# Latent attention by banks of scores, with queries on the partitions of its outputs

## The chip, the core and the metric

One core of a Trainium2 chip runs the whole program. The metric is the device time of one execution in microseconds (us). The kernel before was run three times without a profile and once more with one.

## What is computed

A two-part transformer block on 256 tokens of width 1024, in float32: feed-forward layers, a stick-breaking mixer, cross attention on 256 memory tokens, a state-space mixer, sparse attention. The change lies in the mixer of layer 1 of the first part, a causal attention over latents with 16 heads of 96 query/key features and 64 value features:

```python
def _causal_softmax_attention(q, k, v):
    scale = q.shape[-1] ** -0.5
    def block(args):                      # 128 queries at a time
        q_blk, i = args
        sc = jnp.einsum('bqhd,bkhd->bhqk', q_blk, k) * scale
        causal = k_pos[None, :] <= q_pos[:, None]
        p = jax.nn.softmax(jnp.where(causal, sc, -jnp.inf), axis=-1)
        return jnp.einsum('bhqk,bkhd->bqhd', p, v)
...
def _mla_mixer(...):
    c_q, c_kv, k_r = jnp.split(h @ w_in, ...)
    q = (_rmsnorm(c_q, q_lora_g) @ w_uq)      # 16 heads x 96
    kv = (_rmsnorm(c_kv, kv_lora_g) @ w_ukv)  # 16 heads x (64 + 64)
    ...                                       # norms, rotary part
    return _causal_softmax_attention(q, k, v) @ w_out
```

## The kernel before

Tokens stand in two tiles of 128 (`T` = 0, 1). A weight is loaded as raw float32 (`stage`, DMA on SP's queue), split into a high part on ACT (line 126) and a low part on DVE (line 127), and each product with a weight is three one-pass matmuls (`mm3`, lines 150 to 152). Small products (scores, transposes, probabilities times values) are plain float32 matmuls, which the trace shows as two records for one product and one record for one transpose.

In `mla` the heads go in four chunks of four (`c` = 0 to 3). `heads(c)` makes the chunk's queries, keys and values, `turn` transposes queries and keys (line 858), `attend(c)` is the attention, and `kv(c)` makes one head of the keys and values for the cross attention that follows; it shares nothing with `attend`. `attend(c)` is followed in the program by `heads(c + 1)`, `turn` and `kv(c + 1)`, and at the end come `kv(3)` and `out_linear`, the product with `mla_w_out` (tiles `acc`). The order of instructions on each engine isn't the program's: the tile framework's planner sets it when the program is built, from modelled times and from when buffers come free. So matmuls of `heads`, `kv` and `attend` stand mixed on PE, and each engine then runs its list strictly in that order.

`attend` before, for each `T` and each head `j`: one score product into a PSUM tile of tag C (two of them); DVE adds the mask and takes the row maximum into SBUF tile `s_` (line 920, three buffers); DVE forms minus maximum times scale (line 922); ACT takes the exponential with its row sum (line 924); DVE takes the reciprocal (926) and divides the probabilities (927); `transpose_p` transposes one block (T = 0) or two (T = 1) on PE into a tile of tag B (line 659), and ACT copies it to SBUF (661); one or two products with the values as stationary operand, 64 columns wide, give 64 features by 128 queries in tile `o` (line 931). After four heads `split` writes the high and low parts `oh`, `ol` (lines 192, 193), which `out_linear` reads.

Of the kernel before, what the change touches and what calls it, by code (L numbers as in the profile page):

```python
# [12 lines left out]
AF = mybir.ActivationFunctionType  # L13
ALU = mybir.AluOpType
# [3 lines left out]
P = 128  # L18
# [11 lines left out]
class Net:  # L30
# [743 lines left out]
    def mla(self, fin):  # L774
        nc, tc, a = self.nc, self.tc, self.a
        preps = self.preps()
        w_in, w_uq, w_ukv = a["mla_w_in"][0], a["mla_w_uq"][0], a["mla_w_ukv"][0]
        with tc.tile_pool(name=self.nm("mla"), bufs=1) as pl:
            def T_(shape, name, dt=F32, bufs=1, tag=None):
                return self.lined(pl, shape, dt, tag=tag or name, name=self.nm(name), bufs=bufs)  # L780

            TT = lambda o, x, y, op: nc.vector.tensor_tensor(out=o, in0=x, in1=y, op=op)
# [23 lines left out]
            def cols(T):  # L806
                return slice(T * P, (T + 1) * P)
# [45 lines left out]
            oh, ol = self.o_tiles()  # L853
# [54 lines left out]
                    to_T(qn, qT, T, nc.vector.tensor_copy)  # L908

            def attend(c, qT, kT, vn, rq, *_):  # L910
                for T in range(2):
                    nk = P * (T + 1)
                    po = self.psum(f"D{T + 1}", "o")
                    mask = self.m_c2 if T else self.m_c
                    for j in range(4):
                        sc = self.psum("C", "sc")
                        nc.tensor.matmul(sc[:, 0:nk], qT[:, j, cols(T)], kT[:, j, 0:nk], start=True, stop=True)
                        mx = self.small(2)
                        s_ = T_([P, 256], "s_", bufs=3)
                        nc.vector.tensor_tensor_reduce(out=s_[:, 0:nk], in0=sc[:, 0:nk], in1=mask, scale=1.0, scalar=-3.0e38,  # L920
                                                       op0=ALU.add, op1=ALU.max, accum_out=mx[:, 0:1])
                        nc.vector.tensor_scalar(out=mx[:, 1:2], in0=mx[:, 0:1], scalar1=rq[:, T, j:j + 1], scalar2=-1.0, op0=ALU.mult, op1=ALU.mult)
                        ssum = self.small(1)
                        nc.scalar.activation(s_[:, 0:nk], s_[:, 0:nk], AF.Exp, scale=rq[:, T, j:j + 1], bias=mx[:, 1:2], accum_out=ssum)
                        rec = self.small(1)
                        nc.vector.reciprocal(rec, ssum)
                        nc.vector.tensor_scalar(out=s_[:, 0:nk], in0=s_[:, 0:nk], scalar1=rec, scalar2=None, op0=ALU.mult)
                        pT = self.transpose_p(s_, T + 1, pl, "pT", 2)
                        o = po[(j % 2) * 64:(j % 2) * 64 + 64, (j // 2) * P:(j // 2 + 1) * P]
                        for b in range(T + 1):  # L930
                            nc.tensor.matmul(o, vn[b][:, j, :], pT[:, b, :], start=b == 0, stop=b == T)
                    self.split(po[:, 0:256].rearrange("p (k t) -> p k t", k=2), oh[:, 2 * c:2 * c + 2, cols(T)], ol[:, 2 * c:2 * c + 2, cols(T)])

            kv(0)
            hs = heads(0)
# [1 line left out]
            for c in range(4):  # L937
                attend(c, *hs)
                if c < 3:
                    hs = heads(c + 1)  # L940
                    turn(*hs)
                if c < 2:
                    kv(c + 1)
# [703 lines left out]
```

## Time and profile before

| what | value |
|---|---|
| runs without a profile | 2251.57, 2252.95, 2255.41 us, median 2252.95 |
| profiled execution, its own time | 2254.93 us |
| its span in the trace | 2253.2 us, so 1.73 us lie around the span |
| granted TensorE clock, mean | 0.996 |
| busy, share of the span | PE 98%, PE weight loads 82%, DVE 71%, ACT 57%, POOL 3% |
| stretch with the attention | about 866 to 968.5 us after the span's start |

PE is the matmul unit and PEld its weight loads, which overlap it. A record of PE is longer than the time that it takes in a stream, since the matmuls are pipelined: where the text speaks of a price in a stream, it is the distance from start to start.

### The profile page before, as it was taken

The page shows a single profiled execution, that of the slowest core. Times are in us where ns is not written, and L with a number is a line of the kernel's source. Part 1 is how long each engine was busy: PE and PEld are TensorE (multiplying, and loading weights), DVE is VectorE, ACT ScalarE, POOL GpSimd, SP SyncE. Part 2 cuts the span into 40 slices and gives each one's busy share as a digit, 9 for nine tenths or more (in the row PEclk, how much of TensorE's full clock was granted, in tenths as well). Part 3 has the DMA queues.
Part 4 walks back from the last instruction along what each step waited for, and adds up shares of the span by engine and source line. Part 5 has one row for each costly group of instructions (what it writes and reads, how often), then busy time and mean ns, then how long its engine had stood idle before and what let it go on. Part 6 is the DMA issues. An engine that isn't in the chain of part 4 may idle for free.

```text
span 2253.2 us, 32357 instructions
## 1 busy us (share of the span) xinstructions
PE 2209.4 (98%) x11697; PEld 1842.9 (82%) x11697; DVE 1591.2 (71%) x3496; ACT 1275.7 (57%) x2864; POOL 74.2 (3%) x112
## 2 busy tenths in 40 slices
PE   8999999999999998999999999999999999999999
PEld 6887767788888886777888888887888888778887
DVE  6788666798766677776767656777568565867566
ACT  6755566655665566765554555455555555455553
POOL 0010000000000001100000000000000000000000
PEclk9999999999999999999999999999999999999999
DMA  6775544467567543344565655656555554527552
GB/s 210 240 232 201 179 140 169 134 216 263 183 217 256 194 138 130 119 169 131 176 198 187 207 186 185 241 187 227 187 174 194 196 190 161 178 94 246 187 180 85
DMA packets 280988, 415.94 MB, mean 185 GB/s; under 512 B 18662, under 2 KB 211324, under 8 KB 279804
## 3 DMA queue, kind: packets, MB, share of 16 engines
q1 hardware_dynamic: 275744, 400.87, 53.6%
q10 hardware_dynamic: 5084, 13.00, 1.6%
q8 instruction: 92, 1.51, 0.3%
q14 instruction: 68, 0.56, 0.1%
HBM read 400.07 MB, written 13.76 MB: 184 GB/s over the span
## 4 chain that ended last, share of the span: by engine, by line
PE 83%; DVE 9%; ACT 3%; issue 1%; DMA 1%; POOL 1%; ACTq 0%; SPq 0%; DVEq 0%; POOLq 0%
PE gate L160 11%; PE up L160 11%; PE acc L150 9%; PE acc L151 9%; PE acc L152 9%; PE gate L162 6%; PE up L162 6%; DVE wlo L127 4%; PE proj L152 3%; PE proj L151 3%; PE proj L150 2%; PE up L150 2%; PE up L152 2%; PE up L151 2%; ACT whi L126 1%; PE xT L177 1%
## 5 line engine op out<-in xcount | busy, mean ns | idle before, releaser
L126 ACT ACTIVATE whi<-raw 128x512 fp32r<-128x512 f32 (+1 forms) x1452 | 816.2, 618 | 409.3 <-PE up L160 175.9
L127 DVE TENSOR_TENSOR wlo<-raw,whi 128x512 fp32r<-128x512 f32 (+1 forms) x1452 | 927.7, 678 | 107.1 <-ACT whi L126 69.4
L160 PE MATMUL gate<-x,whi 128*128 128x512 f32 x1200 | 294.0, 392 | 0.0
L160 PE MATMUL up<-x,whi 128*128 128x512 f32 x1200 | 290.6, 390 | 0.1
L150 PE MATMUL acc<-whi,hh 128*128 128x512 f32 x704 | 276.0, 392 | 2.2 <-ACT hh L192 2.2
L151 PE MATMUL acc<-wlo,hh 128*128 128x512 f32 x704 | 275.3, 391 | 0.0
L152 PE MATMUL acc<-whi,hl 128*128 128x512 f32 x704 | 274.5, 390 | 0.0
L167 DVE TENSOR_TENSOR sg<-gate,sg 128x256 f32<-128x256 f32 x150 | 63.5, 423 | 279.8 <-ACT sg L166 279.6
L160 PEld LDWEIGHTS up<-x,whi 128*128 128x128 f32 x1200 | 221.6, 188 | 43.9 <-DVE h L167 0.3
L160 PEld LDWEIGHTS gate<-x,whi 128*128 128x128 f32 x1200 | 221.5, 188 | 44.0 <-DVE sg L167 0.2
L162 PEld LDWEIGHTS gate<-x,wlo 128*128 128x128 f32 x1200 | 157.7, 191 | 8.2
L162 PE MATMUL up<-x,wlo 128*128 128x256 f32 x1200 | 160.5, 283 | 0.0
L162 PE MATMUL gate<-x,wlo 128*128 128x256 f32 x1200 | 160.2, 282 | 0.0
L162 PEld LDWEIGHTS up<-x,wlo 128*128 128x128 f32 x1200 | 154.9, 191 | 4.5
L150 PE MATMUL proj<-whi,x 128*128 128x512 f32 (+2 forms) x400 | 157.7, 394 | 0.1
L151 PE MATMUL proj<-wlo,x 128*128 128x512 f32 (+2 forms) x400 | 155.9, 390 | 0.0
L152 PE MATMUL proj<-whi,x 128*128 128x512 f32 (+2 forms) x400 | 155.1, 388 | 0.4 <-DVE x L193 0.3
L152 PEld LDWEIGHTS acc<-whi,hl 128*128 128x128 f32 x704 | 132.2, 188 | 28.3 <-DVE hl L193 0.4
L150 PEld LDWEIGHTS acc<-whi,hh 128*128 128x128 f32 x704 | 132.5, 188 | 27.8 <-ACT hh L192 2.6
L151 PEld LDWEIGHTS acc<-wlo,hh 128*128 128x128 f32 x704 | 132.5, 188 | 24.5
L360 ACT ACTIVATE sg<-sg 128x256 f32<-128x256 f32 x150 | 62.5, 416 | 81.0 <-DVE sg L297 78.8
L192 ACT ACTIVATE hh<-h 128x512 fp32r<-128x512 f32 x75 | 47.5, 634 | 104.5 <-DVE h L297 104.5
(730 smaller groups left out, 3007.4 us busy)
## 6 DMA issues: line engine op xcount, KB each, us to landing
raw<-in_ffn_w_dram SPq DMA_DIRECT2D x176, 512.0 KB, 4.7
raw<-in_ffn_post_w_gu_dram SPq DMA_DIRECT2D x88, 512.0 KB, 4.8
raw<-in_ffn_w_dram SPq DMA_DIRECT2D x44, 1024.0 KB, 4.9
raw<-in_ffn_pre_w_gu_dram SPq DMA_DIRECT2D x84, 512.0 KB, 5.2
raw<-in_ffn_pre_w_down_dram SPq DMA_DIRECT2D x22, 1024.0 KB, 5.4
raw<-in_ffn_post_w_down_dram SPq DMA_DIRECT2D x22, 1024.0 KB, 4.9
raw<-in_xmem_wkv_dram SPq DMA_DIRECT2D x16, 1024.0 KB, 4.9
raw<-in_sbg_w_in_dram SPq DMA_DIRECT2D x10, 1024.0 KB, 5.1
```

The costliest lines, as they stand in the source:

```text
L126: self.last_hi = nc.scalar.activation(hi[:, s], raw[:, s], AF.Copy)
L127: self.last_lo = nc.vector.tensor_tensor(out=lo[:, s], in0=raw[:, s], in1=hi[:, s].bitcast(F32), op=ALU.subtract)
L150: nc.tensor.matmul(out, xh, wh, start=first, stop=False)
L151: nc.tensor.matmul(out, *a, start=False, stop=False)
L152: nc.tensor.matmul(out, *b, start=False, stop=last)
L160: mm(out, ws(k)[0], x2[:, k].rearrange("p a t -> p (a t)"), start=k == 0, stop=False)
L162: mm(out[:, 256:512], ws(k)[1], x2[:, k, 0, :], start=False, stop=k == n - 1)
L167: self.nc.vector.tensor_tensor(out=d, in0=ps[:, 256:512], in1=d, op=ALU.add)
L177: nc.tensor.transpose(pt[:, j * P:(j + 1) * P], src[:, (b + j) * P:(b + j + 1) * P], self.ident)
L192: self.nc.scalar.activation(hi, src, AF.Copy)
L360: nc.scalar.activation(d, d, AF.Silu)
```

## The change

All of it is in `attend`. Scores of four heads (T = 0, 128 keys each) or two heads (T = 1, 256 keys each) go into one bank of 512 columns: one bank for T = 0 and two for T = 1. Mask and maximum are still taken head by head, the scaled maxima of a bank in one instruction. The exponentials are still one for each head. The probabilities aren't divided; four transposes fill one bank, which one copy of 512 columns moves to SBUF. In the product with the values the probabilities are now the stationary operand (128 columns) and the values move (64 columns), so that `po` has queries on its partitions. Per T there is one reciprocal of four sums and one multiplication of `po` by it into SBUF tile `on`, and `split_T` transposes `on` (two transposes into a tile of tag B) and splits it. `s_` goes from three buffers of 256 columns to two of 512, `pT` from two of 256 to two of 512.

```diff
                 for T in range(2):
                     nk = P * (T + 1)
                     po = self.psum(f"D{T + 1}", "o")
                     mask = self.m_c2 if T else self.m_c
-                    for j in range(4):
+                    ssum = self.small(4)
+                    for j0, n in ((0, 2), (2, 2)) if T else ((0, 4),):
                         sc = self.psum("C", "sc")
-                        nc.tensor.matmul(sc[:, 0:nk], qT[:, j, cols(T)], kT[:, j, 0:nk], start=True, stop=True)
-                        mx = self.small(2)
-                        s_ = T_([P, 256], "s_", bufs=3)
-                        nc.vector.tensor_tensor_reduce(out=s_[:, 0:nk], in0=sc[:, 0:nk], in1=mask, scale=1.0, scalar=-3.0e38,
-                                                       op0=ALU.add, op1=ALU.max, accum_out=mx[:, 0:1])
-                        nc.vector.tensor_scalar(out=mx[:, 1:2], in0=mx[:, 0:1], scalar1=rq[:, T, j:j + 1], scalar2=-1.0, op0=ALU.mult, op1=ALU.mult)
-                        ssum = self.small(1)
-                        nc.scalar.activation(s_[:, 0:nk], s_[:, 0:nk], AF.Exp, scale=rq[:, T, j:j + 1], bias=mx[:, 1:2], accum_out=ssum)
-                        rec = self.small(1)
-                        nc.vector.reciprocal(rec, ssum)
-                        nc.vector.tensor_scalar(out=s_[:, 0:nk], in0=s_[:, 0:nk], scalar1=rec, scalar2=None, op0=ALU.mult)
-                        pT = self.transpose_p(s_, T + 1, pl, "pT", 2)
-                        o = po[(j % 2) * 64:(j % 2) * 64 + 64, (j // 2) * P:(j // 2 + 1) * P]
-                        for b in range(T + 1):
-                            nc.tensor.matmul(o, vn[b][:, j, :], pT[:, b, :], start=b == 0, stop=b == T)
-                    self.split(po[:, 0:256].rearrange("p (k t) -> p k t", k=2), oh[:, 2 * c:2 * c + 2, cols(T)], ol[:, 2 * c:2 * c + 2, cols(T)])
+                        for j in range(n):
+                            nc.tensor.matmul(sc[:, j * nk:(j + 1) * nk], qT[:, j0 + j, cols(T)], kT[:, j0 + j, 0:nk], start=True, stop=True)
+                        mx = self.small(8)
+                        s_ = T_([P, 512], "s_", bufs=2)
+                        for j in range(n):
+                            ks = slice(j * nk, (j + 1) * nk)
+                            nc.vector.tensor_tensor_reduce(out=s_[:, ks], in0=sc[:, ks], in1=mask, scale=1.0, scalar=-3.0e38,
+                                                           op0=ALU.add, op1=ALU.max, accum_out=mx[:, j:j + 1])
+                        nc.vector.scalar_tensor_tensor(out=mx[:, 4:4 + n], in0=mx[:, 0:n], scalar=-1.0, in1=rq[:, T, j0:j0 + n], op0=ALU.mult, op1=ALU.mult)
+                        for j in range(n):
+                            ks = slice(j * nk, (j + 1) * nk)
+                            nc.scalar.activation(s_[:, ks], s_[:, ks], AF.Exp, scale=rq[:, T, j0 + j:j0 + j + 1], bias=mx[:, 4 + j:5 + j],
+                                                 accum_out=ssum[:, j0 + j:j0 + j + 1])
+                        pt = self.psum("B", "pT")
+                        for j in range(4):
+                            nc.tensor.transpose(pt[:, j * P:(j + 1) * P], s_[:, j * P:(j + 1) * P], self.ident)
+                        pT = T_([P, 4, P], "pT", bufs=2)
+                        nc.scalar.activation(pT, pt.rearrange("p (k t) -> p k t", k=4), AF.Copy)
+                        for j in range(n):
+                            for b in range(T + 1):
+                                nc.tensor.matmul(po[:, (j0 + j) * 64:(j0 + j + 1) * 64], pT[:, j * (T + 1) + b, :], vn[b][:, j0 + j, :], start=b == 0, stop=b == T)
+                    rec = self.small(4)
+                    nc.vector.reciprocal(rec, ssum)
+                    on = T_([P, 4, 64], "on", bufs=2)
+                    TT(on, po[:, 0:256].rearrange("p (h d) -> p h d", h=4), rec[:, :, None].to_broadcast([P, 4, 64]), ALU.mult)
+                    self.split_T(on.rearrange("p h d -> p (h d)"), 2, oh[:, 2 * c:2 * c + 2, cols(T)], ol[:, 2 * c:2 * c + 2, cols(T)])
```

## Rows read from the trace of the kernel before

**Rows 1.** The page: busy time of each engine; the chain that ended last.
```profile
PE 2209.4 (98%) x11697; PEld 1842.9 (82%) x11697; DVE 1591.2 (71%) x3496; ACT 1275.7 (57%) x2864; POOL 74.2 (3%) x112
...
PE 83%; DVE 9%; ACT 3%; issue 1%; DMA 1%; POOL 1%; ACTq 0%; SPq 0%; DVEq 0%; POOLq 0%
```

**Rows 2.** Busy time in the attention's stretch: PE, PEld, DVE, ACT, POOL (instructions), clock, DMA.
```profile
866.00:968.50 102.50, 97.32 (x515) 72.60 (x516) 77.12 (x283) 70.77 (x199) 13.76 (x11) 0.98 0.31 106
```

**Rows 3.** Groups by line, 866 to 968.5 us: busy us, mean ns | idle before, releasers.
```profile
L931 PE MATMUL o<-pT,vn 128*64 128x128 f32 x96 | 16.1, 289 | 0.6 <-ACT pT L661 0.4
...
L917 PEld LDWEIGHTS sc<-kT,qT 96*128 96x128 f32 x64 | 10.5, 202 | 2.3 <-DVE sm L920 0.7 <-DVE sm L922 0.5 <-DVE qT L859 0.2
L661 ACT ACTIVATE pT<-pT 128x128 f32<-128x128 f32 (+1 forms) x32 | 10.3, 330 | 11.2 <-PE pT L659 10.7
...
L931 PEld LDWEIGHTS o<-pT,vn 128*64 128x64 f32 x96 | 9.1, 135 | 9.1 <-ACT pT L661 6.9 <-issue 1.1 <-ACT whi L126 0.9
...
L922 DVE TENSOR_SCALAR sm<-sm,rq 128x1 f32<-128x1 f32 x32 | 6.2, 206 | 0.0
...
L926 DVE RECIPROCAL sm<-sm 128x1 f32<-128x1 f32 x32 | 5.1, 159 | 1.2 <-ACT s__1391_8747 L924 0.3 <-ACT s__1671_9715 L924 0.3 <-ACT s__1692_9769 L924 0.2
...
L193 DVE TENSOR_TENSOR ol<-o,oh 128x256 fp32r<-128x256 f32 x8 | 3.4, 420 | 0.7 <-ACT oh L192 0.7
...
L637 PE MATMUL kTm<-ident,kn 128*128 128x128 f32 x10 | 2.1, 289 | 1.6 <-DVE kn L634 1.6
```

**Rows 4.** Line 927 alone in the same stretch: DVE busy (instructions), clock, DMA.
```profile
866.00:968.50 102.50, 10.13 (x32) 0.98 0.31 106
```

**Rows 5.** Timeline of PE, chunk 0, T = 1: start, length, instructions.
```profile
881.97 0.40 PE L150 MATMUL proj<-whi,x 128*128 128x512 f32 x1
882.30 0.65 PE L931 MATMUL o<-pT,vn 128*64 128x128 f32 x4
882.88 0.44 PE L659 MATMUL pT<-ident,s__1377_8711 128*128 128x128 f32 x2
883.08 0.48 PE L151 MATMUL proj<-wlo,x 128*128 128x512 f32 x1
883.39 0.40 PE L152 MATMUL proj<-whi,x 128*128 128x512 f32 x1
883.62 0.40 PE L150 MATMUL proj<-whi,x 128*128 128x512 f32 x1
```

**Rows 6.** Timeline of PE, value products: one alone, eight, and eight of another attention.
```profile
939.83 0.27 PE L931 MATMUL o<-pT,vn 128*64 128x128 f32 x1
...
965.34 1.02 PE L931 MATMUL o<-pT,vn 128*64 128x128 f32 x8
...
2011.17 1.05 PE L1109 MATMUL o<-pT,vn 128*128 128x128 f32 x8
2011.98 0.48 PE L150 MATMUL acc<-whi,oh 128*128 128x512 f32 x1
```

**Rows 7.** Timeline of PE: 64 moving columns (line 503); four transposes (line 177).
```profile
227.74 2.00 PE L503 MATMUL mix<-gn,swT 128*128 128x64 f32 x16 [0.37 <-DVE gn L578]
...
980.44 0.66 PE L177 MATMUL xT<-ident,x 128*128 128x128 f32 x4
```

**Rows 8.** Single lines with min/median/max ns: a 128-column weight load, a 512-column copy.
```profile
L503 PEld LDWEIGHTS mix<-gn,swT x32: 186/192/192, 227.7 to 245.1; 128*128 128x128 f32 x32
...
L522 ACT ACTIVATE qT<-qkT x2: 574/586/599, 258.7 to 265.2; 128x512 f32<-128x512 f32 x2
```

**Rows 9.** Timeline of PE: transposes that waited for divided probabilities.
```profile
875.49 0.30 PE L659 MATMUL pT<-ident,s__1341_8626 128*128 128x128 f32 x1 [1.32 <-DVE s__1341_8626 L927]
...
941.18 0.41 PE L659 MATMUL pT<-ident,s__1584_9445 128*128 128x128 f32 x2 [0.70 <-DVE s__1584_9445 L927]
```

**Rows 10.** Timeline of ACT and of PE: the last `oh` and the first `acc`.
```profile
966.39 0.38 ACT L192 ACTIVATE oh<-o 128x256 fp32r<-128x256 f32 x1 [0.22 <-PE o L931]
```
```profile
968.46 0.39 PE L150 MATMUL acc<-whi,oh 128*128 128x512 f32 x1
```

## The prediction

> **What bounds the kernel now.** I read the page first. PE is busy 98% of the span, and 83% of the chain that ended last is PE's [rows 1]; so an edit counts by what it does to PE's stream, and work taken from DVE or ACT counts only where PE waits for it. Next, the busy times of the stretch that holds `attend`, 866 to 968.5 us: PE 97.3 of 102.5 us, DVE 77.1, ACT 70.8 [rows 2]. The reader should not take 97.3 for useful time. A record lasts longer than its place in a stream: an undisturbed one-pass matmul of 512 columns follows its neighbour after 0.23 us (883.39 to 883.62) and is 0.40 long [rows 5]; a value-product record costs (1.02 − 0.27)/7 = 0.107 us [rows 6], where 0.27 is the length of one record alone [rows 6]. Hence the third view, groups by shape, for the idle time ahead of weight loads, and the fourth, PE's own timeline.
>
> The timeline shows what the averages hide [rows 5]. From 881.97 to 883.39 PE does one large matmul (0.23), four value records (4 × 0.107 = 0.43), two transposes (0.21) and one large matmul (0.23): 1.10 us of work in 1.42 us. The 0.32 us lost lie at seams: 0.10 before the value records (0.33 − 0.23), which wait for ACT's copy; 0.15 after them (0.58 − 0.43); 0.07 to 0.08 after the transposes. The weight loads of line 931 have 9.1 us of idle time ahead of them in the stretch, 6.9 put down to that copy; those of the scores have 2.3 [rows 3]. So what this stretch loses on PE it loses largely at visits of small matmuls between large ones, and the change is about how many visits there are.
>
> **The change, part by part (PE first).** Before there are 8 heads × 4 chunks = 32 visits each for transposes and value products, and up to 32 for scores. After, three banks × 4 chunks = 12 of each, and 8 more for turning `on`.
>
> *Value products.* Before, 32 × (0.10 + 0.15) = 8.0 us of seams; the 9.1 us of idle time ahead of the same loads is the cross-check. After, 12 visits. The 0.15 behind them stands after tiles that use 64 columns of the array; behind the 128-column products of the other attention the next large matmul follows eight records after 0.81 us, no later than 8 × 0.107 [rows 6], so I drop it. The wait ahead I raise from 0.10 to 0.25, because one copy now moves 512 columns, 0.59 us [rows 8] instead of 0.33 on the mean [rows 3]. That leaves 12 × 0.25 = 3.0: a gain of 5.0, with 8.0 as the upper end (no wait left) and below zero as the lower (the slower rival).
>
> *Transposes of the probabilities.* Their number stays 48. Visits go from 32 to 12 + 8 = 20: 12 × 0.07 = 0.8 us gained.
>
> *Scores.* The same matmuls; a bank's scores need no tile to come free between heads. Of the 2.3 us ahead of those loads, 1.2 are put down to DVE's lines 920 and 922, which free the tile; I take 0.7, between 0 and 2.3.
>
> *Added transposes.* 2 × 2 × 4 = 16 records, by the four of line 177 at (0.66 − 0.27)/3 = 0.13 us [rows 7], or 0.107 back to back: 1.7 to 2.1, and I take 1.7 lost, their seams being counted above.
>
> *Turned operands.* The 96 value records now load 128 columns and move 64 where they loaded 64 and moved 128. The nearest row with just that form, line 503, does 16 records in 2.00 us: (2.00 − 0.27)/15 = 0.115 each [rows 7], so 96 × 0.008 = 0.8 lost. If the longer load showed in full it would be (192 − 135) ns × 96 = 5.5 us [rows 8, 3]; the other end is 0.4, from 0.111 at the eight records of line 1109 [rows 6]. I take 0.8, since line 503 is a stream and not a single duration. [...]
>
> *DVE and ACT.* DVE loses 6.2 (line 922) + 5.1 (line 926) [rows 3] + 10.1 (line 927) [rows 4] = 21.4 us and gains 12 × 0.16 (scaled maxima, taken as long as a reciprocal [rows 3]) + 8 × 0.16 + 8 × 0.42 (a 128×256 read of PSUM, as line 193 [rows 3]) = 6.6: 14.8 us of 77.1 less. ACT's copies go from 10.3 [rows 3] to 12 × 0.59 = 7.0 us. The exponentials and maxima stay. All this is under PE's stream, which covers it; it counts only through waits. PE stood 1.6 us ahead of the `kTm` transposes for DVE's `kn`, which queues among the attention's instructions [rows 3]; I take 0.7 of it, between 0 and 1.6. The 1.32 and 0.70 us waits for divided probabilities [rows 9] lose their cause in line 927, but the transposes now wait for the bank's last exponential instead of the head's own; I count nothing, with 2.0 as the upper end. If the cover were gone, DVE's saving would be worth its 14.8 us; nothing in PE's 97.3 says so.
>
> *New waits.* The reciprocal waits for the fourth exponential, the product into `on` for the last value record; behind it on DVE stand `wlo` splits that feed large matmuls. The two new transposes wait on PE for `on`, and whatever the planner put behind them waits too. `s_` has two buffers, so the second bank of T = 1 waits until the transposes of T = 0 have read theirs. No DMA is added or moved. At the end, the last `oh` is written at 966.39 and `acc` starts at 968.46 [rows 10]; its first tile can run chunks 0 to 2, 36 large matmuls or 8 us, before it needs chunk 3, so a last chunk that ends a few us later is covered.
>
> The sum: 5.0 + 0.8 + 0.7 − 1.7 − 0.8 + 0.7 = 4.7 us. The profiled execution took 2254.93 us (span 2253.2 and 1.73 around it) and would take 2250.2; it lies 2.0 above the median, so against 2252.95 the forecast is 2248.2 us, 0.21% less. Everything behind the stretch starts with `acc`, so I see nothing that gives the gain back later.
>
> **Rivals.** *More gain.* PE's waits in the stretch shrink to the upper ends: 8.0 + 0.8 + 2.3 − 1.7 − 0.4 + 1.6 + 2.0 = 12.6 us, 2240.4. For it: DVE has 15 us less in a stretch where it is busy 75% of the time. Against: the copies and exponentials stay in series on ACT.
>
> *No change: the longer weight loads show.* 5.5 instead of 0.8 takes the whole 4.7: 2252.9. For it, the durations; against, line 503's stream [rows 7]. The same time comes out if the waits ahead of the value records grow to 0.64 us a visit (0.25 + 4.7/12), about one 512-column copy.
>
> *Slower: PE blocks at each bank.* PE runs a fixed list. Where a bank's transposes or value products stand too early in it, PE waits for up to four exponentials and a copy, and no large matmul behind them may pass. The two waits of 1.32 and 0.70 us are this mechanism with one head [rows 9]. With 12 banks the change is slower than before by 0.2% once the mean extra wait exceeds (4.7 + 4.5)/12 = 0.77 us a bank; at the 1.32 us already seen it costs 15.8 − 4.7 = 11.1 us, 2264. Against: matmuls of `heads` and `kv` are there to be put between, and a bank has fewer points at which plan and chip can part.
>
> **How the numbers follow.** 0.2%, 4.5 us, is about what a measurement of this kernel can tell from no change. The forecast (gain of 2 to 8 us) has 0.54, and since 4.7 lies hardly above the bound I split it 0.32 faster, 0.22 same. More gain: 0.13, faster. No change: 0.13, same. Slower: 0.20. So 0.45 faster, 0.35 same, 0.20 slower. The range goes to 2240.5, which leaves out a sliver of the second case, and to 2258, which takes in the start of the slower one, up to a mean wait of 0.8 us a bank: some 0.17 is left out. The likeliest case's own range is 2245 to 2251.
>
> **What would show it.** Right: value records in 12 groups of 8 or 16 where the planner lets them, starting about 0.11 us apart; the idle time ahead of their loads falling from 9.1 to about 3 us; lines 922, 926 and 927 gone from DVE, whose busy time in the stretch falls by about 15 us; `acc` beginning some 5 us earlier against the stretch's start. Wrong: single waits of over 0.8 us on PE ahead of transposes or value products in most banks (slower); value records 0.16 us apart (no change); or a stretch that is shorter by 5 us and a span that isn't, which would mean a wait behind 968 that I don't see.

## The result and the profile after

| kernel | runs | median us | range | ratio to the kernel before, 95% interval |
|---|---|---|---|---|
| before, beside the next row | 4 | 2253.15 | 2251.57 to 2255.41 | |
| changed | 4 | 2269.8 | 2268.07 to 2271.52 | 1.0070 [1.0059, 1.0082] |

The change costs 16.7 us, 0.7%: slower, and outside the range forecast. The profiled execution took 2268.07 us, its span is 2266.1. Two lines of the changed kernel's page, the busy times and the chain that ended last:

```profile
PE 2218.0 (98%) x11713; PEld 1852.0 (82%) x11713; DVE 1584.2 (70%) x3428; ACT 1272.6 (56%) x2844; POOL 73.7 (3%) x112
...
PE 83%; DVE 9%; ACT 4%; DMA 2%; issue 1%; POOL 1%; SPq 0%; ACTq 0%; DVEq 0%; POOLq 0%
```

Against [rows 1] DVE is 7.0 us less busy and PE 8.6 us more, with 16 instructions more. The next view is the busy time of the attention's stretch, now 868 to 977 us, and of three pieces of it (columns as in [rows 2]):

```profile
868.00:977.00 109.00, 98.30 (x531) 83.72 (x532) 67.46 (x215) 67.55 (x178) 12.88 (x11) 0.92 0.29 100
...
881.80:885.30 3.50, 3.50 (x15) 3.21 (x15) 2.26 (x8) 2.17 (x6) 0.00 (x0) 0.51 0.25 93
909.20:916.00 6.80, 6.11 (x28) 5.71 (x27) 2.02 (x5) 4.66 (x13) 1.65 (x1) 0.50 0.18 68
946.70:950.10 3.40, 3.40 (x16) 3.40 (x16) 1.03 (x3) 1.94 (x7) 1.39 (x1) 0.50 0.00 0
```

On PE the stretch holds as many records as before and 16 transposes more. DVE's time fell from 77.1 to 67.5 us: line 927 [rows 4] and the waits for it [rows 9] are gone. The granted clock fell from 0.98 to 0.92: beside the spell at the start that both kernels have, PE runs three times at half of the full clock (granted 0.51, 0.50 and 0.50 in the three pieces above), 17.1 us in all with that first spell, where before had 3.4.

The groups of the same stretch, to be held against [rows 3]:

```profile
L939 PE MATMUL o<-vn,pT 128*128 128x64 f32 x96 | 15.3, 313 | 3.6 <-ACT pT L936 3.6
...
L177 PE MATMUL xT<-ident,on 128*128 128x128 f32 x16 | 3.2, 283 | 1.6 <-DVE on L782 1.6
L637 PE MATMUL kTm<-ident,kn 128*128 128x128 f32 x10 | 2.1, 289 | 1.7 <-DVE kn L634 1.7
...
L939 PEld LDWEIGHTS o<-vn,pT 128*128 128x128 f32 x96 | 14.6, 227 | 5.8 <-ACT pT L936 5.6
L920 PEld LDWEIGHTS sc<-kT,qT 96*128 96x128 f32 x64 | 9.8, 200 | 0.9 <-DVE qT L859 0.2
...
L936 ACT ACTIVATE pT<-pT 128x512 f32<-128x512 f32 x12 | 7.2, 597 | 7.7 <-PE pT L934 7.5
L193 DVE TENSOR_TENSOR ol<-xT,oh 128x256 fp32r<-128x256 f32 x8 | 3.3, 416 | 2.2 <-ACT oh L192 2.1
```

Idle time ahead of the value products' weight loads fell from 9.1 to 5.8 us, that ahead of the scores' from 2.3 to 0.9. But PE itself, which stood 0.4 us for the copies before, stands 3.6 us for them and 1.6 us for `on`. The timeline of PE shows where, in chunk 1, and for comparison chunk 3 with the first `acc` (start, length):

```profile
905.93 0.55 PE L934 MATMUL pT<-ident,s__1416_8955 128*128 128x128 f32 x2
907.17 1.10 PE L939 MATMUL o<-vn,pT 128*128 128x64 f32 x8 [0.69 <-ACT pT L936]
908.79 0.44 PE L177 MATMUL xT<-ident,on 128*128 128x128 f32 x2 [0.52 <-DVE on L782]
909.06 0.96 PE L934 MATMUL pT<-ident,s__1426_8991 128*128 128x128 f32 x4
910.71 1.97 PE L939 MATMUL o<-vn,pT 128*128 128x64 f32 x8 [0.69 <-ACT pT L936]
912.47 1.06 PE L934 MATMUL pT<-ident,s__1431_9012 128*128 128x128 f32 x4
913.18 0.67 PE L150 MATMUL q<-whi,cqh 128*128 128x384 f32 x1
...
967.59 1.00 PE L939 MATMUL o<-vn,pT 128*128 128x64 f32 x8
968.40 0.47 PE L152 MATMUL proj<-whi,x 128*128 128x512 f32 x1
...
976.97 0.40 PE L150 MATMUL acc<-whi,oh 128*128 128x512 f32 x1
```

The planner put transposes, value products and turning of a bank one behind the other, with no large matmul between. From 905.93 to 913.18 PE waits three times for what it has just produced to go through ACT or DVE. In that piece the clock drops, and the eight records that take 1.00 us in chunk 3 take 1.97. Chunks 0 and 2 have the same sequence (waits of 0.52 and 0.69 us up to 881.47, of 0.69, 0.52 and 0.69 up to 946.45), each followed by a drop. In chunk 3 `proj` matmuls lie between and there is no wait.

The view of PE's waits in the stretch has one large row besides (us in total, times, longest):

```profile
PE qkT L858 <- DVE qn L782: 3.6, 2, 1.8
PE o L939 <- ACT pT L936: 3.6, 6, 0.7
PE qkT L858 <- ACT whi L126: 3.4, 1, 3.4
PE kTm L637 <- DVE kn L634: 1.7, 4, 0.6
PE xT L177 <- DVE on L782: 1.6, 3, 0.5
```

The third row is the wait ahead of the stretch's first transpose. The others add up to 10.5 us, where before has 4.4. The two waits of 1.8 us stand ahead of the turning of the next chunk's queries; before has none there (the first of these turnings starts at 918.20 before, without a wait):

```profile
925.29 1.05 PE L858 MATMUL qkT<-ident,qn 128*96 128x128 f32 x8 [1.84 <-DVE qn L782]
```

From the last `q` matmul to this turning it takes 5.1 us before (from 913.09) and 5.6 after (from 919.72). Before, value products and transposes of probabilities fill part of that time; after, they have been done earlier and only `proj` and `qkT` matmuls stand in it. No drop of the clock follows either of these two waits.

From the first `qkT` transpose of the stretch (866.61 before, 868.18 after) to the first `acc` (968.46 in [rows 10], 976.97 here) it takes 101.85 us before and 108.79 after. That explains 6.9 of the 12.9 us by which the span grew. The rest, 6.0 us, lies in stages that the diff doesn't touch; it would be larger, had these two executions been at the lower clock equally long there (before for 6.8 us twice, at 26.8 and 1992.9, the changed kernel for 3.4 once, at 195.8). The page's groups of the second feed-forward product, of before and then of the changed kernel (busy us, mean ns):

```profile
L150 PE MATMUL acc<-whi,hh 128*128 128x512 f32 x704 | 276.0, 392 | 2.2 <-ACT hh L192 2.2
L151 PE MATMUL acc<-wlo,hh 128*128 128x512 f32 x704 | 275.3, 391 | 0.0
L152 PE MATMUL acc<-whi,hl 128*128 128x512 f32 x704 | 274.5, 390 | 0.0
```
```profile
L150 PE MATMUL acc<-whi,hh 128*128 128x512 f32 x704 | 279.2, 397 | 1.9 <-ACT hh L192 1.9
L152 PE MATMUL acc<-whi,hl 128*128 128x512 f32 x704 | 279.0, 396 | 0.0
L151 PE MATMUL acc<-wlo,hh 128*128 128x512 f32 x704 | 278.7, 396 | 0.0
```

The same 2112 matmuls got 5 ns longer each, 11.1 us of records. `small(4)` is a new size in the pool of small tiles: 12 buffers of 32 bytes, which move every tile allocated behind it, `hh` among them, by 384 bytes of each partition (`hh` from byte 140800 to 141184). So there are two questions: is the place of the tiles really a cause, and what makes the stretch longer, the edit or the order in which the planner wrote it out?

### The profile page after: what moved, and what is told of

It is laid out like the page before. It is cut to its first block, busy times and chain, and to the rows that moved or that the text cites. A ratio compares the mean times of both kernels' runs of the same rounds, so it can differ in the third digit from the quotient of the medians.

```text
span 2266.1 us, 32261 instructions
## 1 busy us (share of the span) xinstructions
PE 2218.0 (98%) x11713; PEld 1852.0 (82%) x11713; DVE 1584.2 (70%) x3428; ACT 1272.6 (56%) x2844; POOL 73.7 (3%) x112
## 4 chain that ended last, share of the span: by engine, by line
PE 83%; DVE 9%; ACT 4%; DMA 2%; issue 1%; POOL 1%; SPq 0%; ACTq 0%; DVEq 0%; POOLq 0%
PE gate L160 11%; PE up L160 11%; PE acc L150 9%; PE acc L151 9%; PE acc L152 9%; PE gate L162 6%; PE up L162 6%; DVE wlo L127 4%; PE proj L152 3%; PE proj L150 3%; PE proj L151 2%; PE up L152 2%; PE xT L177 2%; PE up L150 2%; ACT whi L126 2%; PE up L151 1%
```

## The experiments

Each ratio is to runs of the kernel before on the same chip (medians 2253.2 to 2254.1 us).

| kernel | median us | ratio, 95% interval | stretch us | half clock, spells that touch it, us |
|---|---|---|---|---|
| before | | | 101.9 | 3.4 |
| changed | 2269.8 | 1.0070 [1.0059, 1.0082] | 108.8 | 17.1 |
| before, moved by 384 bytes | 2263.9 | 1.0046 [1.0033, 1.0058] | 102.1 | 3.4 |
| before, moved by 128 | 2264.1 | 1.0046 [1.0029, 1.0062] | 102.0 | 3.4 |
| before, moved by 256 | 2253.9 | 1.0000 [0.9991, 1.0009] | 101.9 | 3.4 |
| before, moved by 512 | 2253.6 | 1.0000 [0.9991, 1.0008] | 101.8 | 3.4 |
| changed, realigned | 2259.9 | 1.0026 [1.0017, 1.0035] | 108.8 | 17.1 |
| realigned, waits filled | 2260.4 | 1.0027 [1.0018, 1.0037] | 109.2 | 3.4 |
| realigned, copy in halves | 2257.5 | 1.0015 [1.0006, 1.0024] | 105.4 | 10.2 |
| changed, other order | 2251.5 | 0.9989 [0.9980, 0.9998] | 100.6 | 3.4 |
| changed, one bank ahead | 2254.5 | 1.0003 [0.9995, 1.0012] | 104.3 | 6.8 |
| turned outputs only | 2250.6 | 0.9984 [0.9975, 0.9993] | 99.5 | 3.4 |
| banks only | 2248.5 | 0.9977 [0.9962, 0.9992] | (94.1) | 6.8 |
| banks only, heads 0, 2, 1, 3 | 2249.1 | 0.9982 [0.9973, 0.9991] | (94.3) | 3.4 |

Stretch and half clock are read from the one profiled execution of each kernel. The five with the order of before agree (101.8 to 102.1 and 3.4 us), and so do the changed kernel and its realigned form, which have one order (108.8 and 17.1). With banks only, `acc` begins ahead of the last two banks, so those two stretches aren't like the others.

**The place of the tiles.** The kernel before with the pad tile behind the small ones made larger; the order on PE, DVE and ACT stays:

```diff
-        tc.nc.gpsimd.memset(self.pad.tile([P, 24], F32, name="pad"), 0.0)
+        tc.nc.gpsimd.memset(self.pad.tile([P, 120], F32, name="pad"), 0.0)
```

> The kernel before with the pad tile widened by 384 bytes, so that every tile allocated behind it stands where it stands in the changed kernel; the order on PE, DVE and ACT is the same as before. Layout theory (the new size of small tiles moved hh and hl, and matmuls that load them got slower): 8 to 11 us more, 2261 to 2264, and the mean of the acc<-whi,hh records goes from 392 to about 397 ns. Attention theory (all of the loss is in the attention's stretch): 2253, means as before.

It took 10.1 us more and its `acc` groups read as in the changed kernel:

```profile
L150 PE MATMUL acc<-whi,hh 128*128 128x512 f32 x704 | 279.2, 397 | 1.8 <-ACT hh L192 1.8
L152 PE MATMUL acc<-whi,hl 128*128 128x512 f32 x704 | 279.1, 396 | 0.0
L151 PE MATMUL acc<-wlo,hh 128*128 128x512 f32 x704 | 278.5, 396 | 0.0
```

Then the same with `[P, 152]`, `[P, 88]` and `[P, 56]`: 512, 256 and 128 bytes.

> The kernel before with every tile behind the small ones moved by 512 bytes of each partition instead of 384; the instructions and their order are those of the kernel before. Theory A (what costs is that the operands of the three-pass products stand at another place within 512 bytes): no difference, 2251 to 2255 us, and the three lines of acc at 392, 391 and 390 ns as before. Rival B (any move of the tiles costs): 2260 us or more, as for the move by 384.

> The kernel before with the same tiles moved by 256 bytes. Theory A in its plain form (any place other than a multiple of 512 costs the same): 2262 to 2266 us and acc at about 396 ns, as for the move by 384. Rival B (the remainder by 256 or 128 decides, or the move alone): 2251 to 2255 us and acc at 392 ns if 256 is enough.

> The kernel before with the same tiles moved by 128 bytes; moved by 256 and by 512 it took its old time, moved by 384 ten us more. Theory A (an odd multiple of 128 bytes costs, whatever the distance): 2261 to 2267 us, acc at 396 to 397 ns. Rival B (only the remainder 384 of 512, or that one distance, costs): 2251 to 2256 us, acc at 390 to 393 ns.

512 and 256 cost nothing (2253.6 and 2253.9 against 2254.1 us), 128 costs 10 us again (2264.1 against 2253.8). So distance is not what counts, and my plain form, a multiple of 512, fell with the move by 256. What these four moves agree with is an odd multiple of 128 bytes against an even one; no other distance was run.

The counterpart, the changed kernel with the pad at `[P, 56]`, which puts `hh` at an even multiple again (141312) and leaves the order as it was:

> The changed kernel with the pad tile widened by 128 bytes, so that hh and hl start at a multiple of 512 bytes again; order the same as in the changed kernel. Layout theory: 8 to 11 us less than the changed kernel, 2259 to 2262, acc records back at 390 to 392 ns, and the attention's stretch still about 7 us longer than before with its spells of half clock. Attention theory: 2270, no change.

9.9 us came back, the `acc` groups read 393, 392 and 391 ns, and the stretch stayed as it was, clock included. So the place of the tiles is about 10 of the 16.7 us, and 6 remain, in the stretch.

**The edit or its order.** The small tiles of four cut from tiles of eight, a size that the kernel already had:

```diff
-                    ssum = self.small(4)
+                    ssum = self.small(8)[:, 0:4]
...
-                    rec = self.small(4)
+                    rec = self.small(8)[:, 0:4]
```

> The changed kernel whole, with one difference: its two four-wide small tiles are cut from the eight-wide ones that were there before. So no tile moves against the kernel before, and the planner, which counts another set of buffers, writes another order of the same instructions: in chunks 0 and 3, and in parts of 1 and 2, projection matmuls now stand between a bank's transposes, its value products and the turning. Theory A (the edit is sound, and the loss of the realigned changed kernel, 2259.9 us against 2253.8 before, is the planner's order: waits at the hand-offs between the banks and the half clock that follows them): fewer hand-off waits on TensorE between 868 and 975 us, at most one half-clock spell beyond the one at the start of the stretch, and 2245 to 2251 us, for the bank half alone gained 5.3 us and the turning half 3.2. Rival B (banks and turned outputs together are too much, whatever the order): 2257 to 2261 us, half-clock spells as in the realigned one.

Theory A held, though 2251.5 us lies just above its range. The stretch is 8.2 us shorter than in the realigned kernel, with the same instructions in another order. Its timeline in chunk 1:

```profile
904.76 0.38 PE L177 MATMUL xT<-ident,on 128*128 128x128 f32 x2
904.98 0.60 PE L934 MATMUL pT<-ident,s__1426_8991 128*128 128x128 f32 x4
905.34 0.42 PE L151 MATMUL q<-wlo,cqh 128*128 128x384 f32 x1
...
906.33 1.10 PE L939 MATMUL o<-vn,pT 128*128 128x64 f32 x8
```

Five `q` matmuls (the first at 905.34) stand where the changed kernel waited. Over the stretch PE waits 0.9 us for the copies instead of 3.6, and no drop of the clock follows the one at the start. Against the kernel before it is 1.8 us faster by the medians; the interval of the ratio goes from 0.5 to 4.5 us.

**Waits and clock.** Work added into the waits of the realigned kernel, into columns of the output bank that nothing reads, behind each bank's transposes:

```diff
+                        for _ in range(6):
+                            nc.tensor.matmul(po[:, 256:512], cqh[:, 0, 0:P], cqh[:, 1, :], start=True, stop=True)
```

> The realigned changed kernel (2259.9 us) with work added: behind each of the 12 banks' transposes six one-pass matmuls of 256 columns into the unused half of the output bank, whose result nothing reads. They are 72 matmuls of some 0.11 us, 7.7 us of TensorE work in all if nothing covers them. Theory A (waits at the hand-offs and the half clock that follows them): the added work runs in waits that are there anyway, and where it does the granted clock stays up; the time is 2254 to 2262 us, the half-clock spells beyond the first of the stretch fewer than three. Rival B (the stretch is bound by TensorE's own work): the added work comes on top, 2266 to 2269 us.

The whole stretch, realigned and then filled, and what replaced the wait of 0.69 us in chunk 1:

```profile
864.80:973.60 108.80, 98.19 (x531) 83.60 (x532) 67.42 (x214) 67.33 (x177) 12.88 (x11) 0.92 0.30 100
```
```profile
864.70:973.90 109.20, 99.98 (x591) 84.60 (x592) 66.92 (x214) 66.96 (x177) 12.89 (x11) 0.99 0.30 99
```
```profile
905.07 0.60 PE L934 MATMUL pT<-ident,s__1426_9015 128*128 128x128 f32 x4
905.43 0.96 PE L936 MATMUL o<-cqh 128*128 128x256 f32 x6
906.36 1.10 PE L941 MATMUL o<-vn,pT 128*128 128x64 f32 x8
```

The time, 2260.4 us, lies in theory A's range. 60 of the 72 added matmuls lie in the stretch; they start 0.119 us apart (median), 7.1 us of work, and the stretch is 0.4 us longer, so 6.7 us came back. All three later drops of the clock are gone. PE's waits inside the stretch (the view of waits, without the one ahead of its first transpose) add up to 10.7 us in the realigned kernel and to 9.2 in this one, which is 1.5 of it. The other 5.2 agree in size with 13.7 us fewer at half clock, which are worth at most half of that, 6.8. By the same sum the other order comes out: waits of 8.8 us, 1.9 fewer, and 6.8 for the clock are 8.7 against the 8.2 measured. The clock's part is worked out, not measured by itself; and in this run, as in the next, the planner also put some `proj`, `kv` and `q` matmuls elsewhere, so the edit isn't the only difference.

The copy of a bank in two halves, in the realigned kernel:

```diff
-                        nc.scalar.activation(pT, pt.rearrange("p (k t) -> p k t", k=4), AF.Copy)
+                        for k in (0, 2):
+                            nc.scalar.activation(pT[:, k:k + 2, :], pt[:, k * P:(k + 2) * P].rearrange("p (k t) -> p k t", k=2), AF.Copy)
```

> The realigned changed kernel (2259.9 us) with the copy of each bank's turned probabilities cut into two copies of half the width, so that the first value products can start on the first half. Theory A (waits at the hand-off, and the half clock behind them, are what is left of the loss): TensorE waits for the copy less than the 3.6 us over the stretch, fewer half-clock spells, 2254 to 2258 us. Rival B (the hand-off waits are too short to matter): 2259 to 2262 us, 12 copies more and the same spells.

The same place in chunk 1:

```profile
904.27 1.10 PE L940 MATMUL o<-vn,pT 128*128 128x64 f32 x8 [0.47 <-ACT pT L937]
905.89 0.44 PE L177 MATMUL xT<-ident,on 128*128 128x128 f32 x2 [0.52 <-DVE on L782]
906.17 0.60 PE L934 MATMUL pT<-ident,s__1426_8995 128*128 128x128 f32 x4
907.24 0.66 PE L940 MATMUL o<-vn,pT 128*128 128x64 f32 x4 [0.47 <-ACT pT L937]
```

The two waits for the copy are 0.47 instead of 0.69 us and the clock stays up here; drops remain in chunks 0 and 2 (879.2 and 940.6). The stretch is 3.4 us shorter, as much as half of the 6.8 us fewer at half clock. The two intervals of the totals overlap, so this rests on the stretch of one execution of each, and supports the account without showing it.

**One bank ahead.** The layout of before, and the transposes of a bank traced ahead of the value products of the bank before it:

```diff
+                    st.append((T, j0, n, po, ssum, pT))
+                    if len(st) > 1:
+                        finish(c, vn, *st.pop(0))
```

> The change with the layout of before and, traced one bank ahead: the transposes of a bank's exponentials stand in front of the value products, division and turning of the bank before it. Theory A (the loss came from the hand-off of each bank's probabilities right behind their transposes): TensorE has another bank's work at each hand-off, few waits of value products on the copy, no half clock beyond the first spell, 2244 to 2250 us. Rival B (banks and turned outputs together lose whatever the order): 2257 us or more.

Neither theory's time. The waits for copies fell to 1.4 us, but those for `on` rose to 2.0 and those of `qkT` for the next chunk's queries from 3.7 to 4.4: 9.9 us in all. Against the other order, 3.7 us shorter, that is 1.1 more, and a longer spell of half clock at the stretch's start is worth about one more, by estimate from the granted clock (0.97 over 104.3 us, 0.98 over 100.6 in the other order). The rest isn't settled.

**The halves of the change.** Turned outputs head by head (one score product, transposes and copy for each head, as before; division on `on`), and banks with the probabilities divided ahead of the transposes by one product per bank and the old value products:

```diff
-                            nc.tensor.matmul(o, vn[b][:, j, :], pT[:, b, :], start=b == 0, stop=b == T)
+                            nc.tensor.matmul(po[:, j * 64:(j + 1) * 64], pT[:, b, :], vn[b][:, j, :], start=b == 0, stop=b == T)
```
```diff
+                        TT(sv, sv, rec[:, 0:n, None].to_broadcast([P, n, nk]), ALU.mult)
...
+                                nc.tensor.matmul(o, vn[b][:, j, :], pT[:, (j - j0) * (T + 1) + b, :], start=b == 0, stop=b == T)
```

> Scores, exponentials and transposes head by head as before, but values moving, division on the output and turning as in the changed kernel; layout of before. If the turned operand brings the half clock: 2257 to 2261 with half clock in the stretch. If the batching does: 2251 to 2255, half clock only at the stretch's start; the forecast's own terms (seams behind 64-column tiles gone, 16 more transposes) would give 2250 to 2253.

> Scores, exponentials and transposes by banks, but the probabilities are divided before the transposes, the values are the stationary operand again and nothing is turned; no new size of small tiles, so the layout of before. If the 64 moving columns or the turning are what brings the half clock and the waits, the stretch is as before or shorter: 2248 to 2254, half clock only at its start. If the batching brings them (PE waits for a whole bank's exponentials and copy), the stretch is 4 to 8 us longer: 2257 to 2261, with half clock.

Each half gains: 3.2 and 5.3 us, though each also has its own order from the planner, so these are not the edits alone. Neither brings the later drops of the clock, so neither gathering nor turning is by itself what costs. Banks only has the lowest median of all, but its interval overlaps those of turned outputs only and of the other order. Something that I had not priced is at work in it. Value products of before write 64 of the 128 output partitions, even heads the lower half and odd heads the upper. In a bank several heads follow each other directly, and their records start in pairs, 14 ns apart at 964.38 us. To see what that is worth, the banks of T = 1 were made of heads 0 and 2, 1 and 3:

```diff
+                        hd = [(0, 1, 2, 3), (0, 2), (1, 3)][T + j0 // 2]; sc = self.psum("C", "sc")
...
-                        for j in range(j0, j0 + n):
+                        for i in (0, 1) if T else (0, 2, 1, 3):
```

> The kernel with banks only (2248.5 us), with its heads taken in another order: the value products of heads 0 and 2 one behind the other, then 1 and 3, so that neighbouring heads write the same 64 of the 128 output partitions instead of opposite ones. In the run with banks only, the records of two heads start in pairs (964.381 and 964.395 us, then 0.11 us later the next pair), so that a bank's eight end after 0.66 us instead of 1.02. Theory A (heads on opposite halves run side by side, and that is a good part of the gain with banks only): eight records in 1.0 us, 12 banks times 0.36 to 0.42 us, 4 to 5 us more: 2252 to 2254 us. Rival B (the pairs are only how it is recorded, or hidden anyway): 2247 to 2250 us.

A bank of T = 1 with neighbouring heads, and then with heads of one half:

```profile
883.73 0.66 PE L944 MATMUL o<-pT,vn 128*64 128x128 f32 x8
```
```profile
881.29 1.09 PE L944 MATMUL o<-pT,vn 128*64 128x128 f32 x8
```

The pairs are real: without them eight records take 0.43 us longer, in 8 of the 12 banks (at T = 0 a bank still holds heads of both halves, and its eight records still take 0.66). But the time rose by 0.6 us only, inside rival B's range, and the intervals overlap; 3.4 us were to be seen, had PE felt all of it. The two profiled stretches don't settle it: with one half PE waits 1.1 us less in the stretch and spends 2.2 us less of it at half clock, so that their near equality may hide, by estimate, some 2.4 us. What the pairs are worth stays open, since the planner also moved other matmuls in this kernel.

## Why the prediction was wrong

*"The sum" covered `attend` alone.* This is the step that failed first. "Everything behind the stretch starts with `acc`, so I see nothing that gives the gain back later" is refuted: 10 us of the 16.7 lie in stages that the diff doesn't name, because of a tile size in it (`small(4)`) that I read and costed at nothing. Before's trace could not price it; the allocation could have shown that `hh` moves. It is not the only step: realigned, the change still loses 6.1 us (2259.9 against 2253.8).

*New waits.* The slower rival had the mechanism: PE's list put a bank's steps too close together. It was mis-sized. I let it decide only above 0.77 us of extra wait a bank. Measured are 3.6 us for copies and 1.6 for `on`, 5.2 over 12 banks, or 0.43 each, of which the sum had allowed 0.25 already; the other 2.2 us would still have left a gain. None is longer than 0.69 us, so my own sign for this rival, waits of over 0.8 us in most banks, would have called it wrong. The sum lacked two things. One is the 3.6 us that PE waits for `qn` at the next chunk's queries, a place that I didn't name. The other is that the granted clock was down behind three runs of such short waits, for 13.7 us more, by estimate 6.8 us at most. The filled run agrees: with 1.0 us of waits for copies left of 3.6 (those for `on` went from 1.6 to 2.8), none of the three later spells came, and the granted clock over the stretch was 0.99 instead of 0.92. What lowers the clock is not shown.

*Value products, scores, transposes.* Borne out in kind. Idle time ahead of the value loads fell (9.1 to 5.8, not to 3), ahead of the scores' by 1.4 (0.7 forecast). In the order with few hand-off waits the change gained 1.8 us where 4.7 were forecast. There PE waits 8.8 us in the stretch against 4.4 before, at the same half clock, and the stretch is still 1.3 us shorter, so PE's own work in it takes some 5.6 us less: the fewer visits gave about what I forecast for the whole, and new waits took most of it back.

*Turned operands.* Right: the longer loads (227 ns on the mean, 135 before) don't show in the spacing. Eight records in 1.00 us are (1.00 − 0.27)/7 = 0.104 us apart, so they hide, and the turned half alone gains. (From the second record on they start 0.111 us apart; the first gap is shorter.) The comparison was with the wrong partner, though: the next large matmul starts 0.81 us after the first of eight turned records (967.59 to 968.40), and with banks only, where the old form pairs, 0.60 us after it (964.38 to 964.98).

*DVE and ACT.* DVE fell by 9.7 us in a window 6.5 us longer; 14.8 were forecast. The `kTm` waits for `kn`, of which I took 0.7 back, stayed (1.6 and 1.7).

The parts add up: place of the tiles 10 (2263.9 against 2253.8), order 8.4 (2259.9 against 2251.5), the edit −1.8: 16.6 of 16.7 us.

## What to carry to other kernels

Before costing an edit stage by stage, look at what it does to the addresses of tiles that it doesn't touch: here a new small tile in a pool raised the price of a hot loop elsewhere by 10 us, and padding to the old places is a one-line test. When work is gathered into larger steps, ask what PE has to do between one step's production and its use; here the gain from fewer visits was lost where the planner left the steps back to back (2259.9 us, and 2251.5 in the other order). And try the halves of a compound change alone: here each of them beat the whole as it was first built.

## What the runs showed of the hardware

In the `acc` products `hh` and `hl` are the stationary operands; the weight tiles that move through them are allocated ahead of the small tiles and stayed where they were. With `hh` and `hl` moved by 384 bytes of a partition, a matmul record of 512 columns took 5 to 6 ns more (390 to 392 before, 396 to 397 then) and the kernel 10.1 us more (2263.9 against 2253.8); moved by 128 bytes the kernel took 10.3 us more, and moved by 256 or 512 no more, with records of 390 to 393 ns. The loads before them stayed (188 ns before, 189 in the changed kernel). Products with neither operand moved hardly changed, as `gate` shows, before and with the move by 384 bytes:

```profile
L160 PE MATMUL gate<-x,whi 128*128 128x512 f32 x1200 | 294.0, 392 | 0.0
```
```profile
L160 PE MATMUL gate<-x,whi 128*128 128x512 f32 x1200 | 295.3, 393 | 0.0
```

Which access pays is not shown.

Value products of two heads that fill opposite halves of the 128 output partitions started in pairs. In the run with banks only, records of two heads start 14 ns apart at 964.38 us, the next pair 0.16 us later, and the others every 0.11 us, so that eight end after 0.66 us; where neighbouring heads fill the same half, eight took 1.09 us (881.29). Why they pair is not shown. The kernel before had shown it once, where one head's records end and the next head's begin: of the eight at 965.34 [rows 6] the fourth and the fifth start 12 ns apart (965.703 and 965.715).
